# Hybrid decoder layer on one core: the fourth weight sum of a block pair moved to GpSimd, and the first key rotation moved ahead of a value block

## The chip, the core and the metric

The kernel runs on 1 core of one Trainium2 chip. A core has TensorE (PE in the profile; its weight loads are PEld), VectorE (DVE), ScalarE (ACT), GpSimd (POOL) and SyncE (SP), 16 DMA engines, an on-chip memory (SBUF) of 128 partitions and an accumulator memory (PSUM) that TensorE writes. The metric is the device time of one execution in microseconds (us), the median over several runs.

## The reference

One layer on 256 tokens of 2048 features, all in fp32. The change touches two places of it: how the weights of any large product are brought to TensorE, and the rotary step on the keys.

```python
hn = rmsnorm(h, norm_mix_w)
q, k, v, g_ret, xr, yr, g_a, g_b = split(hn @ w_in)
q = rotary(q, positions); k = rotary(k, positions) * 128 ** -0.5     # 8 heads of 128
ret = head_groupnorm(chunkwise_retention(q, k, v), ret_gn_w)         # 8 value heads of 256
ret_out = silu(g_ret) * ret
rnn_out = gelu(yr) * rg_lru(causal_dwconv(xr), ...)
merged = sigmoid(g_a) * (ret_out @ w_proj_ret) + sigmoid(g_b) * (rnn_out @ w_proj_rnn)
h = h + merged @ w_mix_out
h = h + memory_cross_attention(rmsnorm(h), rmsnorm(mem), xa_w_q, xa_w_k, xa_w_v, xa_w_o)
h = h + conv_gated_ffn(rmsnorm(h), ffn_w_up, ffn_w_down)             # inner width 5632
out = rmsnorm(h, final_norm_w)
```

## The kernel before, in words

**Weights.** Every weight matrix comes from memory in tiles of 128 partitions x 2048 numbers (four 128-row blocks by 512 columns, 1 MB). `prefetch` (L247) runs over one long list of weight units, two units ahead of the products that use them. For a unit it loads the tile (`raw`, L264, a DMA of the SP queue; six buffers), lets ACT round it to a high half (`hi`, L285) and lets DVE subtract that from the tile to get the low half (`lo`, L286); there are three buffers of each half. TensorE then multiplies with both: high activations by high weights (L361), low activations by high weights (L362), and high activations by low weights (L368), so it needs the low half only after the products with the high half.

**Pairs.** Where a product has two neighbouring 512-column blocks, `pair_products` (L384) does half of it with seven block products in place of eight, in the manner of Strassen and Winograd. Its eleven units stand in `PAIR_UNITS` (L102) in the order q1, p0, q3, p1, q5, q2, q6, p2, q7, q4, p3. The q units are the seven products; their weights are sums of tiles that are built in place, in three held tiles called A, B and C. The p units are ordinary products for the other half of the rows. The sums are:

- q1 loads A, q3 loads B, q2 loads C.
- For q5 a DMA from the POOL queue adds a tile from memory onto A (L266, an accumulating transfer). A is split into halves for q5.
- Behind that split DVE does A += B (L293, the third weight sum), and A is split again for q6.
- For q7 another accumulating DMA of the POOL queue (L266) adds a tile onto B. It has to wait for A += B, which reads B.
- Behind q6's split an entry is put into the list `after`; the next unit to be prefetched, p2, emits **A += C** (L291, the fourth weight sum) behind its own split. A is then split for q4.

There are 20 such pairs, so L291 and L293 run 20 times each, on tiles of 128 x 2048. The two last stretches of pairs are the down projections of the feed-forward layer (`pair_add`, L423). In the first pair of each, part of the activations is still being finished (`hidden`, L1260, ending in a split by ACT at L550 and DVE at L551) while its products already run.

**The first group.** The retention works on two groups of four heads (loop at L830). For group 0 the order in the code is: queries' product, value block 0 (`gemm_n`, L848), rotation of the queries (`rotated`, L708), split of value block 0 (`split_rows`, L557); then keys' product, four sums of the input (`sum_x`, L815, one behind each of the first units of the next product), value block 1, rotation of the keys, split of value block 1; then the pair of gate blocks. A rotation is eight DVE instructions (two of L715, four of L717, two of L721) and two splits (ACT L547, DVE L548). The rotated keys go to `retain` (L755), whose scores are small products (L517). A value block lies in PSUM until `split_rows` has read it (ACT L562, DVE L563); there are three such accumulators, and a pair needs all three.

**What sets the order.** Each engine works through its own queue in order. The queues are filled by a scheduler when the program is made: it takes the order of the code as priority and may put an instruction that is ready earlier ahead of one that isn't. Buffers of a pool are handed out in the order of the code.

Of the kernel before, what the change touches and what calls it, by code (L numbers as in the profile page):

```python
# [13 lines left out]
ALU = mybir.AluOpType  # L14
# [139 lines left out]
def hybrid_layer(  # L154
# [16 lines left out]
    act, dve, pe, pool, sp = nc.scalar, nc.vector, nc.tensor, nc.gpsimd, nc.sync  # L171
# [13 lines left out]
    def nm(s):  # L185
        count[0] += 1
        return f"{s}_{count[0]}"

    def big(shape, dt=F32, s="b"):
        return bp.tile(shape, dt, tag="big", name=nm(s))  # L190

    def tmp(s="t"):
        return tp.tile([P, 2, S], F32, tag="tmp", name=nm(s))
# [45 lines left out]
    def load_x(n):  # L239
        while len(xin) < n:  # L240
            t = big([P, 2, BW], s="nat")
            rows = x[0].rearrange("(t p) d -> p t d", p=P)
            c = len(xin) * BW
            act.dma_start(out=t, in_=rows[:, :, c : c + BW])
            xin.append(t)

    def prefetch(n):  # L247
        while len(ahead) < n and taken[0] < len(stream):
            kind, slot, op, i = stream[taken[0]]
            src = None if i is None else wall[i]  # L250
            taken[0] += 1
            first = taken[0] == 1
            if op == "new":
                raw = wp.tile([P, KC, BW], F32, tag="raw", bufs=RAW_BUFS, name=nm("raw"))
                if slot:
                    held[slot] = raw
            else:
                raw = held[slot]
            if taken[0] <= 4:
                xs.load(2 * taken[0] - 1)  # L260
            pieces = ((0, 1), (1, 2), (2, 4)) if first else ((0, 2), (2, 4)) if taken[0] <= 3 else ((0, 4),)
            for a, b in pieces:
                if op == "new":
                    sp.dma_start(out=raw[:, a:b, :], in_=src[:, a:b, :])  # L264
                elif op == "add":
                    pool.dma_start(out=raw, in_=src, accum_op=ALU.add)  # L266
                if first and a == 0:
                    sp.dma_start(out=xs.rest[0], in_=xs.rest[1])
                elif first and a == 1 or a == 0 and taken[0] <= 4:
                    xs.load(2 * taken[0])  # L270
            if taken[0] == 5:
                sp.dma_start(out=cid, in_=consts[:, 0:C_DEC])
                sp.dma_start(out=pa[:, 16:P], in_=by_feature[:, 16:P])
                sp.dma_start(out=pb, in_=by_feature[:, P : P + 80])
            if taken[0] == 7:
                sp.dma_start(out=pf.rearrange("p a n -> p (a n)"), in_=by_feature[:, P + 80 :])
            hi = wp.tile([P, KC, BW], F32R, tag="hi", bufs=PART_BUFS, name=nm("hi"))
            lo = wp.tile([P, KC, BW], F32R, tag="lo", bufs=PART_BUFS, name=nm("lo"))
            for a, b in pieces:
                if taken[0] <= 4:  # L280
                    xs[2 * (taken[0] - 1) + (b - 1) // KH]
                if first and b <= KH:
                    dve.tensor_copy(hi[:, a:b], raw[:, a:b])  # L283
                else:
                    act.copy(hi[:, a:b], raw[:, a:b])  # L285
                dve.tensor_tensor(  # L286
                    out=lo[:, a:b], in0=raw[:, a:b], in1=hi[:, a:b].bitcast(F32), op=ALU.subtract
                )
            if after:
                to, by = (held[i] for i in after.pop())  # L290
                dve.tensor_tensor(out=to, in0=to, in1=by, op=ALU.add)  # L291
            if kind == "q5":
                dve.tensor_tensor(out=raw, in0=raw, in1=held["B"], op=ALU.add)  # L293
            elif kind == "q6":
                after.append(("A", "C"))
            parts = [(hi[:, k : k + KH], lo[:, k : k + KH]) for k in range(0, KC, KH)]
            ahead.append((kind, parts))
            if taken[0] >= 4:
                load_x(min(4, 2 * (taken[0] - 3)))
# [3 lines left out]
    def later(n, fn):  # L303

        pending.append((step[0] + n + 1, fn))
# [64 lines left out]
    def gemm_n(w, row, st, nk, col):  # L370

        a = acc()
        for k0, parts in chunks(nk, w, row, col):
            ops = [
                [halves(st[(k0 + k) // 2], (k0 + k) % 2, slice(tt * P, (tt + 1) * P)) for k in range(KC)]
                for tt in range(2)
            ]
            for tt in range(2):
                upper_n(a[:, tt, :], ops[tt], parts, k0 == 0)
            for tt in range(2):  # L380
                lower_n(a[:, tt, :], ops[tt], parts, k0 + KC >= nk)
        return a
# [151 lines left out]
    def joined(a, s="j"):  # L534

        c = tmp("c")
        o = tmp(s)
        with tc.high_priority(URGENT):
            act.copy(c, a[:, :, S:BW])  # L539
            dve.tensor_tensor(out=o, in0=a[:, :, 0:S], in1=c, op=ALU.add)  # L540
        return o

    def split_pair(src, scale=None):

        t = big([P, 2, BW], F32R, s="s")
        if scale is None:
            act.copy(t[:, :, 0:S], src)  # L547
            dve.tensor_tensor(out=t[:, :, S:BW], in0=src, in1=t[:, :, 0:S].bitcast(F32), op=ALU.subtract)  # L548
        else:
            act.mul(t[:, :, 0:S], src, scale)  # L550
            dve.scalar_tensor_tensor(  # L551
                out=t[:, :, S:BW], in0=src, scalar=scale, in1=t[:, :, 0:S].bitcast(F32),
                op0=ALU.mult, op1=ALU.subtract,
            )
        return t

    def split_rows(a, r):  # L557

        hi, lo = (big([P, 2, BW], F32R, s="v") for _ in range(2))
        for tt in range(2):  # L560
            c = r[:, tt : tt + 1]
            act.mul(hi[:, tt, :], a[:, tt, :], c)  # L562
            dve.scalar_tensor_tensor(  # L563
                out=lo[:, tt, :], in0=a[:, tt, :], scalar=c, in1=hi[:, tt, :].bitcast(F32),
                op0=ALU.mult, op1=ALU.subtract,
            )
        return hi, lo
# [140 lines left out]
    def rotated(qs_):  # L708

        o = []  # L710
        cb = cos[:, None, :].to_broadcast([P, 2, S])
        for pr in range(2):
            q = qs_[pr]
            ta, tb = tmp("ta"), tmp("tb")
            dve.tensor_tensor(out=ta, in0=q, in1=cb, op=ALU.mult)  # L715
            for lo_, hi_ in ((0, 64), (64, 128)):
                dve.tensor_tensor(  # L717
                    out=tb[lo_:hi_], in0=q[64 - lo_ : 128 - lo_],
                    in1=sin[64 - lo_ : 128 - lo_, None, :].to_broadcast([64, 2, S]), op=ALU.mult,
                )  # L720
            dve.tensor_add(ta, ta, tb)  # L721
            o.append(split_pair(ta))
        return o
# [91 lines left out]
    def sum_x(i):  # L815

        t = tmp("xt")
        sp.dma_start(out=t, in_=x_t[:, 2 * i : 2 * i + 2, :])
        for j in range(2):
            act.activation(t[:, j, :], t[:, j, :], AF.Identity, scale=p_mix(2 * i + j))  # L820
        xs_sums.append(sums(t))
# [8 lines left out]
    for g in range(2):  # L830
        dec = big([P, 4, S], s="dec")
        vs, turned = [], []
        for b, o in enumerate((O_Q, O_K)):
            a = qjoin if g == b == 0 else [joined(t, "q") for t in gemm_t("w_in", 0, xs, NT, o + g * BW)]
            if b == 0:
                sp.dma_start(
                    out=dec,
                    in_=consts[:, C_DEC + g * 4 * S : C_DEC + (g + 1) * 4 * S].rearrange("p (h s) -> p h s", s=S),
                )
            if g > 0:  # L840
                turned.append(rotated(a))
                if b == 0:
                    vs += [split_rows(v, rs0) for v in pair_out("w_in", xs, xs_sums, O_V + 1024)]
            else:
                if b == 1:
                    for i in range(KC):
                        later(i, lambda i=i: sum_x(i))
                v = gemm_n("w_in", 0, xs, NT, O_V + b * BW)  # L848
                turned.append(rotated(a))
                vs.append(split_rows(v, rs0))  # L850
        qr, kr = turned
        gates = [head_gate(a, big([P, 2, BW], s="gate")) for a in pair_out("w_in", xs, xs_sums, O_G + g * 1024)]
        retain(g, qr, kr, vs, dec, gates)
# [418 lines left out]
    for part, nb_ in enumerate(FF_PARTS):  # L1272
# [18 lines left out]
        if final:  # L1291
            wfin = []
            for i in range(2):
                t = big([P, 2, BW], s="wf")
                sp.dma_start(
                    out=t.rearrange("p a n -> p (a n)"),
# [48 lines left out]
```

## Time and profile before

| | us |
|---|---|
| median of 3 runs (2005.9 to 2008.41) | 2006.04 |
| the profiled execution, as timed | 2005.55 |
| its span, first to last instruction | 2003.8 |
| PE busy | 1988.4 (99%) |
| DVE busy | 1583.4 (79%) |
| ACT busy | 1157.9 (58%) |
| POOL busy | 47.0 (2%) |
| DVE in the 20 sums of L291 | 45.8 |

Between the profiled execution's span and its time lie 1.75 us. A row of the trace gives the start, the duration, the engine, the line of the kernel, the operation, the tile written and the tiles read (`lo<-raw,hi`), the shape, and in square brackets how long the engine stood idle just before and what it waited for. Consecutive rows of an engine overlap by some hundredths of a microsecond. PE's matmuls are pipelined, so the duration of one (0.39) is longer than the distance between two starts (0.23 for 512 columns).

### The profile page before, as it was taken

How to read it: one execution, taken by the hardware profiler on the slowest of the kernel's cores; microseconds unless marked ns; L12 is line 12 of the kernel's file. 1: busy time of each engine (PE TensorE's matmuls, PEld its weight loads, DVE VectorE, ACT ScalarE, POOL GpSimd, SP SyncE). 2: the span in 40 equal slices, each digit the busy share in tenths (PEclk: the TensorE clock that was granted, in tenths of full speed). 3: DMA queues.
4: the chain of work that ended last, by engine and by line, in shares of the span. 5: the costliest groups of instructions: out<-in, count | busy, mean ns of one | idle time of the engine just before them, and what ended most of it. 6: DMA issues, size and time to landing. Idle time of an engine off the chain costs nothing.

```text
span 2003.8 us, 24972 instructions
## 1 busy us (share of the span) xinstructions
PE 1988.4 (99%) x10072; PEld 1692.9 (84%) x10072; DVE 1583.4 (79%) x1588; ACT 1157.9 (58%) x1167; POOL 47.0 (2%) x52
## 2 busy tenths in 40 slices
PE   9999999999999999999999999999999999999998
PEld 8878888888888888888888888888888888888887
DVE  6798797789985876778888768777797787886775
ACT  6565656767665554566666656555554554544552
POOL 0001000000000000000000000000000000000000
PEclk9999999999999999999999999999999999999999
DMA  9764675555887675777886748754678555684561
GB/s 370 259 214 135 235 257 179 210 190 157 266 261 261 210 252 183 248 257 234 267 259 206 258 126 231 264 198 174 207 233 275 196 192 216 204 290 178 204 237 64
DMA packets 79460, 443.57 MB, mean 221 GB/s; under 512 B 8688, under 2 KB 13424, under 8 KB 31600
## 3 DMA queue, kind: packets, MB, share of 16 engines
q1 hardware_dynamic: 72064, 397.39, 53.9%
q0 software_dynamic: 5760, 41.95, 11.2%
q10 hardware_dynamic: 1520, 2.63, 0.4%
q8 instruction: 79, 1.29, 0.3%
q14 instruction: 37, 0.30, 0.0%
HBM read 425.16 MB, written 16.78 MB: 221 GB/s over the span
## 4 chain that ended last, share of the span: by engine, by line
PE 91%; DVE 3%; issue 2%; DMA 2%; ACT 1%; POOLq 0%; SPq 0%; ACTq 0%; POOL 0%; DVEq 0%
PE acc L350 38%; PE acc L361 16%; PE acc L368 16%; PE acc L362 16%; DMA raw<-in_wall 2%; PE sm L517 2%; DVE lo L286 1%; PE sm L529 1%; PE acc L517 1%; ACT hi L285 1%; PE sm L894 1%; DVE raw L293 0%; DVE tb L717 0%; DVE ta L721 0%; DVE fv L1192 0%
## 5 line engine op out<-in xcount | busy, mean ns | idle before, releaser
L286 DVE TENSOR_TENSOR lo<-raw,hi 128x2048 fp32r<-128x2048 f32 (+1 forms) x420 | 951.0, 2267 | 295.0 <-ACT hi L285 288.1
L285 ACT CAST hi<-raw 128x2048 fp32r<-128x2048 f32 (+1 forms) x418 | 793.2, 1902 | 615.5 <-PE acc L362 274.2
L361 PE MATMUL acc<-hi,s 128*128 128x512 f32 x1336 | 522.6, 391 | 2.0 <-DVE v L563 1.6
L362 PE MATMUL acc<-hi,s 128*128 128x512 f32 x1336 | 520.7, 390 | 0.4 <-DVE s L551 0.4
L350 PE MATMUL acc<-s,hi 128*128 128x512 f32 x2176 | 519.3, 392 | 1.1 <-DVE hi L283 1.1
L350 PEld LDWEIGHTS acc<-s,hi 128*128 128x128 f32 x2176 | 402.7, 189 | 80.9 <-issue 1.4
L368 PE MATMUL acc<-lo,s 128*128 128x512 f32 x1336 | 340.0, 392 | 0.0
L361 PEld LDWEIGHTS acc<-hi,s 128*128 128x128 f32 x1336 | 250.9, 188 | 54.6 <-DVE v L563 2.0
L368 PEld LDWEIGHTS acc<-lo,s 128*128 128x128 f32 x1336 | 250.1, 188 | 53.3
L362 PEld LDWEIGHTS acc<-hi,s 128*128 128x128 f32 x1336 | 250.9, 188 | 52.2 <-DVE s L551 1.1
L350 PEld LDWEIGHTS acc<-s,lo 128*128 128x128 f32 x2176 | 277.7, 192 | 8.8 <-DVE lo L286 0.4
L350 PE MATMUL acc<-s,lo 128*128 128x256 f32 x2176 | 282.9, 284 | 0.0
L361 PE MATMUL acc<-hi,ss 128*128 128x512 f32 x320 | 126.4, 395 | 1.8 <-ACT o L453 1.5
L362 PE MATMUL acc<-hi,ss 128*128 128x512 f32 x320 | 124.8, 390 | 0.0
L368 PE MATMUL acc<-lo,ss 128*128 128x512 f32 x320 | 86.0, 390 | 0.0
L539 ACT COPY c<-acc 128x512 f32<-128x512 f32 x68 | 39.4, 581 | 70.3 <-PE acc L350 69.9
L361 PEld LDWEIGHTS acc<-hi,ss 128*128 128x128 f32 x320 | 60.1, 188 | 16.0 <-ACT o L453 2.0
L266 POOL DMA_DIRECT2D raw<-in_wall x40 | 35.2, 879 | 1570.3 <-DVE lo L286 999.0
L368 PEld LDWEIGHTS acc<-lo,ss 128*128 128x128 f32 x320 | 60.0, 188 | 12.7
L362 PEld LDWEIGHTS acc<-hi,ss 128*128 128x128 f32 x320 | 60.1, 188 | 12.1
L426 DVE TENSOR_TENSOR nat<-nat,acc 128x512 f32<-128x512 f32 (+1 forms) x49 | 43.9, 908 | 5.1 <-PE acc L368 5.1
L291 DVE TENSOR_TENSOR raw<-raw,raw 128x2048 f32<-128x2048 f32 x20 | 45.8, 2288 | 0.4
(233 smaller groups left out, 1241.8 us busy)
## 6 DMA issues: line engine op xcount, KB each, us to landing
raw<-in_wall SPq DMA_DIRECT2D x333, 1024.0 KB, 4.9
raw<-in_wall POOLq DMA_DIRECT2D x40, 1024.0 KB, 7.9
fkept<-nat SPq DMA_DIRECT2D x12, 512.0 KB, 7.5
nat<-fkept SPq DMA_DIRECT2D x12, 512.0 KB, 5.8
xt<-in_x_t SPq DMA_DIRECT2D x11, 256.0 KB, 6.5
raw<-in_wall SPq DMA_DIRECT2D x5, 512.0 KB, 7.9
nat<-in_x ACTq DMA_DIRECT2D x4, 512.0 KB, 10.0
ret<-hd SPq DMA_DIRECT2D x8, 256.0 KB, 4.1
```

The lines of the kernel that those rows point to most:

```text
L266: pool.dma_start(out=raw, in_=src, accum_op=ALU.add)
L285: act.copy(hi[:, a:b], raw[:, a:b])
L286: dve.tensor_tensor(out=lo[:, a:b], in0=raw[:, a:b], in1=hi[:, a:b].bitcast(F32), op=ALU.subtract)
L291: dve.tensor_tensor(out=to, in0=to, in1=by, op=ALU.add)
L350: pe.matmul(a, part, sx, start=k == 0 and t == 0, stop=k == nk - 1 and t == 0, skip_group_check=True)
L361: pe.matmul(o, h, hi, start=start and kk == 0, stop=False, skip_group_check=True)
L362: pe.matmul(o, l, hi, start=False, stop=False, skip_group_check=True)
L368: pe.matmul(o, h, lo, start=False, stop=stop and kk == KC - 1, skip_group_check=True)
L426: dve.tensor_tensor(out=o, in0=o, in1=i, op=op)
L517: pe.matmul(o, a, b, start=start and i == 0, stop=stop and i == 2, skip_group_check=True)
L529: pe.transpose(t[:, j, tt * P : (tt + 1) * P], rows[:, tt, k + j * P : k + (j + 1) * P], ident)
L539: act.copy(c, a[:, :, S:BW])
```

## The change

Two edits. The first gives the fourth weight sum, A += C, to GpSimd in place of VectorE, in all 20 pairs; its operands and its place in the code stay. The second lets group 0 rotate its keys right behind their product, ahead of the four input sums and of value block 1's product, where before the rotation stood behind that product. The queries of group 0 stay where they are.

```diff
@@ -288,7 +288,7 @@
             if after:
                 to, by = (held[i] for i in after.pop())
-                dve.tensor_tensor(out=to, in0=to, in1=by, op=ALU.add)
+                pool.tensor_tensor(out=to, in0=to, in1=by, op=ALU.add)
             if kind == "q5":
                 dve.tensor_tensor(out=raw, in0=raw, in1=held["B"], op=ALU.add)
@@ -843,10 +843,12 @@
             else:
                 if b == 1:
+                    turned.append(rotated(a))
                     for i in range(KC):
                         later(i, lambda i=i: sum_x(i))
                 v = gemm_n("w_in", 0, xs, NT, O_V + b * BW)
-                turned.append(rotated(a))
+                if b == 0:
+                    turned.append(rotated(a))
                 vs.append(split_rows(v, rs0))
```

## The prediction

> **What bounds the kernel now.** I read the page first, for which engine has no room.
>
> ```profile
> span 2003.8 us, 24972 instructions
> ...
> PE 1988.4 (99%) x10072; PEld 1692.9 (84%) x10072; DVE 1583.4 (79%) x1588; ACT 1157.9 (58%) x1167; POOL 47.0 (2%) x52
> ...
> L286 DVE TENSOR_TENSOR lo<-raw,hi 128x2048 fp32r<-128x2048 f32 (+1 forms) x420 | 951.0, 2267 | 295.0 <-ACT hi L285 288.1
> ...
> L291 DVE TENSOR_TENSOR raw<-raw,raw 128x2048 f32<-128x2048 f32 x20 | 45.8, 2288 | 0.4
> ...
> raw<-in_wall POOLq DMA_DIRECT2D x40, 1024.0 KB, 7.9
> ```
>
> PE is busy for 1988.4 of 2003.8 us, so all its idle time is 15.4 us; a change that does no less PE work can gain no more than the part of it that it removes. DVE has 79%: the 20 sums of L291 are 45.8 us of an engine that isn't the bound. Next I read PE's busy time by stretches: the first pair, two pairs in the middle, and the first pair of each of two down projections.
>
> ```profile
> core 0: us, PE busy (x) PEld busy (x) DVE busy (x) ACT busy (x) POOL busy (x), PEclk, DMA share, GB/s
> 96.60:143.30 46.70, 43.01 (x193) 35.25 (x193) 43.08 (x40) 28.25 (x26) 0.87 (x1) 1.00 0.60 203
> 645.70:686.50 40.80, 40.80 (x182) 33.78 (x180) 34.10 (x19) 25.21 (x20) 1.72 (x2) 1.00 0.68 211
> 686.50:727.30 40.80, 40.80 (x182) 33.78 (x180) 37.62 (x24) 26.98 (x24) 0.87 (x1) 1.00 0.76 247
> 1451.60:1493.70 42.10, 41.67 (x182) 33.64 (x181) 39.81 (x35) 26.56 (x21) 1.76 (x2) 1.00 0.69 227
> 1713.00:1754.90 41.90, 41.65 (x183) 33.63 (x182) 39.80 (x35) 26.57 (x21) 1.76 (x2) 1.00 0.67 230
> ```
>
> The middle pairs have PE busy in every microsecond (40.80 of 40.80): nothing can be gained there, only lost. The first pair has 46.70 - 43.01 = 3.69 us of idle PE, the largest block in the kernel behind the start. The two down pairs have 0.43 and 0.25, and DVE at 95% (39.81 of 42.10).
>
> **The change part by part: the keys.** The first pair's waits on PE are these three.
>
> ```profile
> start us, us, engine line op out<-in xcount [idle before <-releaser]
> 109.06 1.12 PE L517 MATMUL sm<-s,s 128*128 128x256 f32 x8 [0.89 <-DVE s L548]
> ...
> 111.37 0.50 PE L361 MATMUL acc<-hi,ss 128*128 128x512 f32 x1 [1.20 <-ACT o L453]
> ...
> 113.32 1.07 PE L368 MATMUL acc<-lo,ss 128*128 128x512 f32 x4
> ...
> 115.99 0.50 PE L361 MATMUL acc<-hi,s 128*128 128x512 f32 x1 [1.60 <-DVE v L563]
> ```
>
> Their sum is 0.89 + 1.20 + 1.60 = 3.69, all the idle time of that stretch. Counted by starts it is a little more: the four matmuls from 113.32 go 0.23 apart, the next was due at 114.2 and came at 115.99, 1.8 for the third. I take 4.0 for the three. All three go back to DVE:
>
> ```profile
> 78.31 0.68 DVE L540 TENSOR_TENSOR q<-acc,c 128x512 f32<-128x512 f32 x1
> ...
> 100.45 0.68 DVE L715 TENSOR_TENSOR ta<-q,cos 128x512 f32<-128x512 f32 x1
> ...
> 101.37 1.38 DVE L717 TENSOR_TENSOR tb<-q,sin 64x512 f32<-64x512 f32 x2
> ...
> 103.40 0.68 DVE L721 TENSOR_TENSOR ta<-ta,tb 128x512 f32<-128x512 f32 x1
> ...
> 108.32 0.68 DVE L548 TENSOR_TENSOR s<-ta,s 128x512 fp32r<-128x512 f32 x1
> ...
> 115.19 0.74 DVE L563 SCALAR_TENSOR_TENSOR v<-acc,ro,v 128x512 fp32r<-128x512 f32 x1
> ```
>
> The keys are complete at 78.99, and their rotation begins at 100.45, behind the four input sums. It costs 2 x (0.68 + 1.38 + 0.68 + 0.68) = 6.8 us of DVE between 100 and 112.4, ahead of value block 1's split, whose last instruction ends at 115.93; at 115.99 the matmul that wants that accumulator starts. The first wait is for rotated keys; the second is for an ACT copy (L453) that stands behind the keys' casts in ACT's queue. With the rotation ahead of the value block its 6.8 us fall between 73 and 96.6:
>
> ```profile
> 72.90:96.60 23.70, 23.70 (x110) 19.78 (x109) 14.54 (x20) 13.09 (x14) 1.04 (x1) 1.00 0.73 226
> ```
>
> DVE is idle there for 23.70 - 14.54 = 9.2 us, so the 6.8 fit, and PE has no wait in it. If that cover were thinner, a low half would come late by at most the 2.3 us that two rotation steps hold it back. No DMA moves with the rotation; the ones it now stands ahead of are the four loads of the input sums. Behind it nothing else is late: the accumulator is read some 7 us earlier. Term: **-4.0**, bounds -4.2 and 0.
>
> **The change part by part: the sums.** Removed from DVE: 20 x 2.29 us, worth nothing to PE in pairs where PE doesn't wait. Added to POOL: 20 adds of 128 x 2048, which no row shows. Two things are unknown, how long one takes and whether it gets in DVE's way. The nearest row by operation and shape is DVE's own, 2.29; on POOL the trace has only small powers:
>
> ```profile
> 193.93 5.85 POOL L609 TENSOR_TENSOR ro<-rv,mhalf 128x8 f32<-128x8 f32 x1 [3.87 <-DVE rv L607]
> ...
> 327.96 1.82 POOL L609 TENSOR_TENSOR ro<-rv,mhalf 128x8 f32<-128x8 f32 x1 [72.13 <-DVE rv L607]
> ...
> 900.79 0.72 POOL L609 TENSOR_TENSOR ro<-rv,mhalf 128x2 f32<-128x2 f32 x1 [1.31 <-DVE rv L607]
> ```
>
> From two columns to eight the power grows by 1.1 us, 0.18 a column; by that a sum would last 380 us and every pair would take ten times as long. A power is another operation than an add, so I leave that end out of the range and take 2.29, with twice that, one pass for each of the two inputs, as the upper bound. The same rows tell of the second unknown: the same power took 1.82 once and 5.85 the other time. In the long case DVE ran this:
>
> ```profile
> 193.75 2.28 DVE L286 TENSOR_TENSOR lo<-raw,hi 128x2048 fp32r<-128x2048 f32 x1
> 195.96 2.28 DVE L291 TENSOR_TENSOR raw<-raw,raw 128x2048 f32<-128x2048 f32 x1
> 198.98 2.29 DVE L286 TENSOR_TENSOR lo<-raw,hi 128x2048 fp32r<-128x2048 f32 x1 [0.74 <-ACT hi L285]
> ```
>
> Two instructions with two SBUF inputs, back to back until 198.24, then 0.74 idle; POOL ended at 199.78, 1.54 after they had ended. So POOL gets its inputs only when DVE pauses. I assume the reverse as well, that DVE's two-input work waits for a POOL add under way; no row shows it.
>
> [...]
>
> What a sum costs in a middle pair:
>
> ```profile
> 662.39 2.29 DVE L286 TENSOR_TENSOR lo<-raw,hi 128x2048 fp32r<-128x2048 f32 x1 [1.38 <-ACT hi L285]
> 664.72 2.29 DVE L291 TENSOR_TENSOR raw<-raw,raw 128x2048 f32<-128x2048 f32 x1
> 666.93 2.29 DVE L286 TENSOR_TENSOR lo<-raw,hi 128x2048 fp32r<-128x2048 f32 x1
> ...
> 669.51 1.92 ACT L285 CAST hi<-raw 128x2048 fp32r<-128x2048 f32 x1 [0.16 <-PE acc L362]
> ...
> 675.62 0.39 PE L361 MATMUL acc<-hi,ss 128*128 128x512 f32 x1
> ```
>
> q6's low half ends at 664.68. On POOL the sum then ends at 666.97, or at 669.26 if it takes twice as long; q4's cast starts at 669.51 either way, since it waits for PE to free a buffer. p2's low half starts between 666 and 669.3 in place of 666.93, and the halves are some 5 us ahead of PE (q7's is cast at 667.4, its products start at 675.62). Cost 0. The accumulating transfer for q7 is not held up: it needs A += B only, which q6's split needs too, so it is ready before the sum and I expect it ahead in POOL's queue. Behind the sum POOL has nothing until the next pair's transfer.
>
> The exceptions are the first down pairs:
>
> ```profile
> 1473.97 2.28 DVE L286 TENSOR_TENSOR lo<-raw,hi 128x2048 fp32r<-128x2048 f32 x1
> 1477.36 0.69 DVE L551 SCALAR_TENSOR_TENSOR s<-fo,s 128x512 fp32r<-128x512 f32 x1 [1.10 <-ACT s L550]
> ...
> 1735.35 2.28 DVE L286 TENSOR_TENSOR lo<-raw,hi 128x2048 fp32r<-128x2048 f32 x1
> 1738.56 0.69 DVE L551 SCALAR_TENSOR_TENSOR s<-fo,s 128x512 fp32r<-128x512 f32 x1 [0.93 <-ACT s L550]
> ...
> 1739.31 0.50 PE L362 MATMUL acc<-hi,s 128*128 128x512 f32 x1 [0.22 <-DVE s L551]
> ```
>
> PE waits for this L551 already (1739.31 follows 1739.25). DVE's pause ahead of it begins at 1737.63; a POOL sum that takes the pause ends at 1739.92 and pushes L551 from 1738.56 by 1.36. At 1476.25 likewise: 1478.54 - 1477.36 = 1.18. Cost **+2.5**, bounds 0 (nothing held) and 7.1 (twice the length: 3.65 + 3.47).
>
> Sum: -4.0 + 2.5 = -1.5 on the profiled execution's 2005.55 (1.75 around its span of 2003.8; 0.5 under the median of 2006.04): **2004.0**. A measurement here tells about 0.2%, 4 us, from no change; this is within.
>
> **The rivals.** *Nothing held:* POOL's add runs beside DVE and only the rotation counts: 2005.55 - 4.0 = 2001.5, at the edge of faster. For it: no row shows DVE held by POOL (the split at 198.98 lasted 2.29 though the power ended at 199.78). Against it: the 5.85.
>
> *The add takes twice DVE's row and holds DVE:* -4.0 + 7.1 = +3.1, 2008.6. It turns to slower by over 4 us from an add of about 5 us (both stalls then 4 each), and beyond 6 the middle pairs' cover goes too: p2's low half would end past 673 in a pair that needs it about then. For it: a power needs 0.7 us for two columns, so POOL isn't quick.
>
> *The transfer behind the sum (slower):* the place is POOL's queue. If the sum stands ahead of q7's transfer, as it does in the code, the transfer starts at 666.97, lands 7.9 later at 674.87, is cast until 676.79 and its low half is ready at 679.1, against products due at 675.62 and, with the low half, eight matmuls (1.8) later: 1.7 late. It decides as soon as the order is this one. In 18 of the 20 pairs (two have scores among their products and more room) that is 18 x 1.7 = 30 us at least: 2032 or more. Against it: DVE's queue has L291 at 664.72 ahead of p2's split at 666.93, against the code's order, so what is ready goes first.
>
> *The rotation doesn't move:* then -4.0 falls away and 2008 remains; the 6.8 us of cover speak against it.
>
> **How the numbers follow.** Forecast 0.32; nothing held 0.27; twice as long and held 0.24, a third of it past 4 us; transfer behind the sum 0.10; rotation without gain 0.07. Faster by over 0.2%: most of nothing held and a little of the forecast, 0.28. Slower: the transfer, a third to a half of the long add, some of the last, and stalls of the queues' new order that I can't see, 0.34. Within: 0.38. The range goes from 2000.8 (nothing held, -4.2 and the half microsecond of the down pairs) to 2016, an add of 6 us (4.8 + 5.1 in the down pairs by the same steps, and an estimated 5 in the middle pairs with the least cover: 2005.55 - 4.0 + 14.9); the transfer's case stays outside.
>
> **What would show it.** Right: no idle PE between 105 and 118, L715 at 73 to 90, accumulating transfers ahead of sums on POOL. The length of L291 on POOL and of L286 beside it decide between forecast and rivals: L286 rows over 2.3 us mean that DVE is held. PE's wait for L551 at the two down pairs gives the price. Wrong: PE waits at q7 or q4 in middle pairs, casts that wait for transfers, or new waits in the first 100 us.

## The result and the profile after

The changed kernel takes 2034.08 us, the median of 4 runs (2032.57 to 2039.62), against 2005.97 for the kernel before beside it: a ratio of 1.0143, 95% interval 1.0122 to 1.0164. It is slower by 28 us, where 2004.0 was forecast, and the range ended at 2016. The profiled execution lasted 2033.99 us.

The page of the changed kernel, its span, the engines' busy time and the two groups of DVE's low halves and of the moved sum (instructions x count, then busy us, mean ns, idle us before them):

```profile
span 2032.2 us, 24977 instructions
...
PE 1999.9 (98%) x10072; PEld 1699.4 (84%) x10072; DVE 1598.3 (79%) x1568; ACT 1157.6 (57%) x1167; POOL 151.7 (7%) x72
...
L286 DVE TENSOR_TENSOR lo<-raw,hi 128x2048 fp32r<-128x2048 f32 (+1 forms) x420 | 989.8, 2362 | 306.8 <-ACT hi L285 298.4
...
L291 POOL TENSOR_TENSOR raw<-raw,raw 128x2048 f32<-128x2048 f32 x20 | 106.6, 5331 | 92.8 <-DVE lo L286 89.0
```

Three readings. A sum takes 5.33 us on POOL instead of 2.29 on DVE. DVE gave up 45.8 us of sums and is busier than before, 1598.3 against 1583.4: its other instructions became longer by 60.7. And PE, with the same 10072 matmuls, is busy for 11.5 us more (1999.9 - 1988.4) and idle for 16.9 more (32.3 against 15.4). The two make up the 28.4 by which the span grew. So there are two losses: TensorE waits, and for some time it works more slowly.

The view of PE's waits of the changed kernel says for whom (total, times, longest):

```profile
PE acc L362 <- DVE s L551: 6.6, 2, 3.4
PE acc L361 <- ACT ss L505: 3.2, 1, 3.2
PE sm L529 <- ACT hd L752: 2.6, 1, 2.6
...
PE acc L368 <- DVE lo L286: 1.8, 1, 1.8
```

**A POOL sum and DVE's work with two SBUF inputs exclude each other.** Rows of the changed kernel's timeline, first a sum that found DVE idle, with the low half that started 0.59 us later:

```profile
721.03 4.61 POOL L291 TENSOR_TENSOR raw<-raw,raw 128x2048 f32<-128x2048 f32 x1 [2.97 <-DVE lo L286]
...
721.62 6.17 DVE L286 TENSOR_TENSOR lo<-raw,hi 128x2048 fp32r<-128x2048 f32 x1 [0.68 <-ACT hi L285]
...
941.21 4.61 POOL L291 TENSOR_TENSOR raw<-raw,raw 128x2048 f32<-128x2048 f32 x1 [3.65 <-DVE lo L286]
...
941.36 4.62 DVE L503 TENSOR_TENSOR sm<-xt,sm 128x128 f32<-128x128 f32 x1
```

The sum ends at 725.64, the low half at 727.79: 2.15 later, about its usual 2.28. It did nothing while the sum ran. The second couple is plainer: a DVE add of 128 columns, 0.28 to 0.29 us in the kernel before, needs 4.62, to just behind the sum's end. The other order:

```profile
268.16 2.28 DVE L286 TENSOR_TENSOR lo<-raw,hi 128x2048 fp32r<-128x2048 f32 x1
...
268.33 6.62 POOL L291 TENSOR_TENSOR raw<-raw,raw 128x2048 f32<-128x2048 f32 x1 [3.03 <-DVE lo L286]
...
123.09 4.86 POOL L291 TENSOR_TENSOR raw<-raw,raw 128x2048 f32<-128x2048 f32 x1 [10.54 <-DVE lo L286]
...
123.39 0.74 DVE L786 BATCH_NORM_STATS2 bn<-rc 128x6 f32<-128x256 f32 x2
```

Where DVE is first, POOL waits: the sum of 268.33 lasts 6.62 and ends 4.5 behind the low half. The statistics at 123.39, which have one input, run inside a sum in their usual 0.41 each. The sum's own length is thus 4.6 (the shortest of the 20 is 4.60, the median 4.63).

**Half clock.** In the first pair of the first down projection (PE's, POOL's and DVE's rows, then busy time by stretches, where the sixth number is the granted clock):

```profile
1492.23 7.11 POOL L291 TENSOR_TENSOR raw<-raw,raw 128x2048 f32<-128x2048 f32 x1 [5.65 <-DVE lo L286]
...
1496.21 3.68 DVE L551 SCALAR_TENSOR_TENSOR s<-fo,s 128x512 fp32r<-128x512 f32 x1 [1.26 <-ACT s L550]
...
1499.95 0.50 PE L362 MATMUL acc<-hi,s 128*128 128x512 f32 x1 [3.22 <-DVE s L551]
...
1501.43 0.63 PE L361 MATMUL acc<-hi,s 128*128 128x512 f32 x1
1501.86 0.63 PE L362 MATMUL acc<-hi,s 128*128 128x512 f32 x1
```
```profile
1500.90:1504.30 3.40, 3.40 (x10) 2.66 (x9) 3.40 (x3) 0.45 (x2) 0.00 (x0) 0.51 0.92 383
1504.30:1508.00 3.70, 3.70 (x17) 3.02 (x17) 2.39 (x3) 1.84 (x1) 0.00 (x0) 0.99 1.01 427
```

DVE is ready for L551 at 1496.21, the sum holds it until 1499.34, and TensorE waits 3.2 us. Behind that the matmuls start 0.43 apart instead of 0.23, for 3.4 us, at a granted clock of 0.51. The trace's clock record has five such stretches inside the kernel after, each 3.41 us or twice that, 23.9 us in all, and none before. At half speed that is about 12 us of work, the 11.5 of PE's busy time.

**Two more places.** In the second pair (at 170 in the kernel before) the power of the retention's norm stands behind the sum in POOL's queue; its result is wanted by the gate, the heads and TensorE in turn:

```profile
197.18 6.66 POOL L291 TENSOR_TENSOR raw<-raw,raw 128x2048 f32<-128x2048 f32 x1 [3.79 <-DVE rv L607]
203.80 3.73 POOL L609 TENSOR_TENSOR ro<-rv,mhalf 128x8 f32<-128x8 f32 x1
...
207.56 0.36 DVE L798 TENSOR_SCALAR ro<-ro,ro 128x4 f32<-128x4 f32 x2 [0.97 <-POOL ro L609]
...
216.00 1.38 PE L529 MATMUL sm<-cid,rc 128*128 128x128 f32 x8 [2.65 <-ACT hd L752]
```

It ended at 207.53, in the kernel before at 199.78. Of these 7.75 us the first pair had already lost 3.3; the other 4.4 are the sum's. And in the pair at 476, four scans that stood behind four low halves more in DVE's queue before (at 516.47, 2.43 us for the four) now stand ahead of p2's low half, where room had come, and are held by POOL:

```profile
509.77 5.62 POOL L291 TENSOR_TENSOR raw<-raw,raw 128x2048 f32<-128x2048 f32 x1 [7.61 <-DVE lo L286]
...
510.93 6.76 DVE L919 TENSOR_TENSOR_SCAN xr<-aa,ti 128x256 f32<-128x256 f32 x4
...
518.19 2.28 DVE L286 TENSOR_TENSOR lo<-raw,hi 128x2048 fp32r<-128x2048 f32 x1
...
520.53 1.88 PE L368 MATMUL acc<-lo,s 128*128 128x512 f32 x5 [1.80 <-DVE lo L286]
```

**The keys.** The loads of the input sums on SP's queue, the last of these sums, and TensorE in the first pair, all of the kernel after:

```profile
64.72 14.28 SPq L264 DMA_DIRECT2D raw<-in_wall  x4
79.05 0.43 SPq L818 DMA_DIRECT2D xt<-in_x_t  x1
...
89.63 0.68 DVE L548 TENSOR_TENSOR s<-ta,s 128x512 fp32r<-128x512 f32 x1
90.23 0.28 DVE L500 TENSOR_TENSOR sm<-xt 128x128 f32<-128x128 f32 x1
...
112.03 0.69 DVE L506 TENSOR_TENSOR ss<-sm,ss 128x512 fp32r<-128x512 f32 x1 [0.15 <-ACT ss L505]
...
108.39 0.49 PE L362 MATMUL acc<-hi,ss 128*128 128x512 f32 x1 [0.57 <-DVE ss L506]
112.05 0.80 PE L361 MATMUL acc<-hi,ss 128*128 128x512 f32 x1 [3.16 <-ACT ss L505]
```
```profile
111.70:118.50 6.80, 6.45 (x15) 4.76 (x16) 5.45 (x8) 4.26 (x6) 0.86 (x1) 0.50 0.79 149
```

The rotation runs where it was forecast, 79.2 to 90.3, and the old waits for L548, L453 and L563 are gone. But the input sums begin only behind it, at 90.23 (82.88 before), their loads start at 79.05 in place of 72.28, and the fourth sum is complete at 112.72 rather than 103.47. The two rows of the kernel before:

```profile
72.28 0.43 SPq L818 DMA_DIRECT2D xt<-in_x_t  x1
...
102.78 0.69 DVE L506 TENSOR_TENSOR ss<-sm,ss 128x512 fp32r<-128x512 f32 x1
```

q3, the pair's third product, multiplies with these sums (`ss`): 3.7 us of waits again, now followed by 6.8 us at half clock.

How much later the same matmul starts than in the kernel before, by stretches of that kernel's time (us gained or lost within each; the experiments' columns are used below):

| stretch, in the time of the kernel before | after | `sum_only` | `sum_pieces` | `sum_spared` | `sum_eleven` |
|---|---|---|---|---|---|
| start and first pair, to 169.5 | 3.3 | 0.3 | -0.2 | 0.2 | 1.7 |
| second pair, to 237 | 6.1 | 5.9 | 7.6 | 5.9 | 0.5 |
| third pair, to 306 | 1.3 | 1.3 | 1.7 | 1.3 | 0.3 |
| pairs at 476 to 602, to 645.7 | 4.0 | 5.3 | 6.2 | 7.6 | 0.0 |
| to 905 | 0.0 | 0.0 | 1.0 | 0.0 | 0.0 |
| to 1036 | 1.1 | 0.5 | 4.4 | 1.0 | 0.0 |
| pairs of two cross-attention products, to 1180 | 2.8 | 3.0 | 7.8 | 2.9 | 0.0 |
| to 1451.6 | 0.0 | 0.0 | 2.1 | 0.0 | 0.0 |
| first down projection, to 1535 | 4.0 | 5.0 | 2.2 | -0.3 | -0.3 |
| second down projection, to the end | 5.5 | 5.7 | 2.7 | 0.5 | 0.5 |
| all | 28.2 | 27.1 | 35.5 | 19.2 | 2.7 |

### The profile page after: what moved, and what is told of

Read it like the earlier page. It is cut to its first block, busy times and chain, and to the rows that moved or that the text cites. A ratio compares the mean times of both kernels' runs of the same rounds, so it can differ in the third digit from the quotient of the medians.

```text
span 2032.2 us, 24977 instructions
## 1 busy us (share of the span) xinstructions
PE 1999.9 (98%) x10072; PEld 1699.4 (84%) x10072; DVE 1598.3 (79%) x1568; ACT 1157.6 (57%) x1167; POOL 151.7 (7%) x72
## 4 chain that ended last, share of the span: by engine, by line
PE 87%; DVE 6%; issue 3%; DMA 2%; ACT 1%; POOL 1%; SPq 0%; POOLq 0%; ACTq 0%; DVEq 0%
PE acc L350 36%; PE acc L361 16%; PE acc L362 16%; PE acc L368 16%; DVE lo L286 2%; DMA raw<-in_wall 1%; PE sm L517 1%; ACT hi L285 1%; PE sm L529 1%; PE sm L896 1%; PE acc L517 0%; DVE raw L293 0%; DVE s L551 0%; POOL raw L291 0%; DVE xr L919 0%
## 5 line engine op out<-in xcount | busy, mean ns | idle before, releaser
L286 DVE TENSOR_TENSOR lo<-raw,hi 128x2048 fp32r<-128x2048 f32 (+1 forms) x420 | 989.8, 2362 | 306.8 <-ACT hi L285 298.4
L291 POOL TENSOR_TENSOR raw<-raw,raw 128x2048 f32<-128x2048 f32 x20 | 106.6, 5331 | 92.8 <-DVE lo L286 89.0
L368 PEld LDWEIGHTS acc<-lo,ss 128*128 128x128 f32 x320 | 60.7, 190 | 13.0
```

What stands on the lines that cost most here:

```text
L286: dve.tensor_tensor(out=lo[:, a:b], in0=raw[:, a:b], in1=hi[:, a:b].bitcast(F32), op=ALU.subtract)
L291: pool.tensor_tensor(out=to, in0=to, in1=by, op=ALU.add)
L368: pe.matmul(o, h, lo, start=False, stop=stop and kk == KC - 1, skip_group_check=True)
```

## The experiments

The theory: the sum on POOL and DVE's two-input work exclude each other, and what is late by it costs in a few pairs, with half clock behind the longer waits; the keys' rotation makes the input sums late. The rivals: the loss is the sum's own lateness or POOL's slowness; it runs through all pairs; the clock drops for another reason than idling; the rotation's place itself is at fault.

**`sum_only`: the first edit alone.**

```diff
-                dve.tensor_tensor(out=to, in0=to, in1=by, op=ALU.add)
+                pool.tensor_tensor(out=to, in0=to, in1=by, op=ALU.add)
```

> The fourth weight sum on GpSimd alone, the keys rotated where they were before. Theory (hold): one add of 4.6 us keeps out every VectorE instruction with two SBUF inputs while it runs, so this part costs most of the change: about 23 us over before, near 2029 us. It shows low-half splits stretched from 2.28 to 5 or 6 us, waits of TensorE for L551 of some 3.5 us in the first pair of each down projection, and half-clock stretches behind them. Rival (the two edits meet): the loss needs both edits in the first pairs, and the sums alone cost the two down pairs only, about 10 us, 2016 us.

2033.03 us (2032.08 to 2035.34), ratio 1.0132, 1.0115 to 1.0149. That is 4 us more than worked out, and far from the rival's 2016: the sum is nearly the whole loss. The two waits for L551 are the same as after (6.3 us together).

**`keys_only`: the second edit alone** (the second part of the change's diff).

> The keys rotated ahead of value block 1 alone, sums on VectorE. Theory (late input sums): the rotation takes the place of the four input sums in the queues and buffers, the fourth input sum comes some 9 us later, TensorE waits for it at the third product of the first gate pair: about 5 us slower than before, 2011 us. Rival (the forecast's step): the three waits of 3.7 us vanish, 4 us faster, 2002 us, and what was seen in the first pair of the changed kernel came from the sums on GpSimd.

2008.84 (2008.31 to 2009.52), ratio 1.0010, 1.0001 to 1.0020. A small loss, just clear of the noise and smaller than worked out, in place of a gain of 4. The two losses added are 26.36 + 2.17 = 28.5 us, against 28.1 for both edits together.

**`keys_xtbig`: the second edit, the input tiles of the sums in another buffer pool**, so that their loads don't wait for a small temporary.

```diff
-        t = tmp("xt")
+        t = big([P, 2, BW], s="xt")[:, :, 0:S]
```

> As the keys alone, but the four input tiles of the input sums lie in the pool of large buffers and not among the ten temporaries that the rotation uses. If the input sums are late because their loads wait for a temporary behind the rotation's, the loads start as before (72 to 84 us), the fourth input sum is ready by about 105 us and the time is 4 us under before, 2002 us. If it is VectorE's time and queue order that delays them, the time stays near that of the keys alone, 2011 us.

2009.55 (2008.74 to 2012.24), ratio 1.0015, 1.0006 to 1.0025. The last input sum starts at 112.21, no earlier. The buffer isn't what holds the loads back. They stand behind one weight load more in SP's queue (the x4 above was x3 in the kernel before), and the sums' DVE part stands behind the rotation.

**`sums_then_keys`: the second edit, the input sums hung into the keys' own product**, one product earlier.

```diff
+            if g == 0 and b == 1:
+                for i in range(KC):
+                    later(i, lambda i=i: sum_x(i))
             a = qjoin if g == b == 0 else [joined(t, "q") for t in gemm_t("w_in", 0, xs, NT, o + g * BW)]
...
                 if b == 1:
-                    for i in range(KC):
-                        later(i, lambda i=i: sum_x(i))
+                    turned.append(rotated(a))
                 v = gemm_n("w_in", 0, xs, NT, O_V + b * BW)
-                turned.append(rotated(a))
+                if b == 0:
+                    turned.append(rotated(a))
```

> Sums on VectorE; the four input sums behind the first units of the keys' own product, the keys' rotation ahead of value block 1. Theory (late input sums): with the input sums out of the way the rotation's place is worth what was forecast: no wait of TensorE between 105 and 118 us, about 4 us faster than before, 2002 us. Rival (VectorE has no room): the work only moves, VectorE's splits for value block 1 come late, no gain or a loss.

2001.57 (2001.25 to 2003.68), ratio 0.9974, 0.9963 to 0.9984: faster than both kernels. The stretch of the first pair, the last rotated keys and the last input sum:

```profile
96.60:143.30 46.70, 46.70 (x214) 38.96 (x213) 38.93 (x23) 29.22 (x22) 0.87 (x1) 1.00 0.80 250
```
```profile
88.23 0.69 DVE L506 TENSOR_TENSOR ss<-sm,ss 128x512 fp32r<-128x512 f32 x1
...
97.27 0.69 DVE L548 TENSOR_TENSOR s<-ta,s 128x512 fp32r<-128x512 f32 x1
```

PE is busy in all of the 46.70 us. This is the gain of 4 that was forecast for the keys.

**`sums_early_keys_late`: the input sums as there, the rotation where it was**, behind value block 1 (of that diff the three lines that hang in the input sums, and their old three lines taken out; the rotation's lines stay as in the kernel before).

> The sums on DVE. The four input sums are put into the keys' own product, as in the faster version of the keys' part, but the rotation of the keys stays behind value block 1, where it was. If the gain of that version comes from the rotation's place, this one gains nothing: 2005.5 to 2007. If it comes from the input sums being out of the rotation's way (in the kernel before, the rotation begins at 100.45 only because the last input sum ends there), most of the gain is here too: 2001.5 to 2003.5, and the waits for L548 and L563 are gone with the rotation still in its old place.

2001.84 (2001.12 to 2003.87), ratio 0.9980, 0.9971 to 0.9990. The same gain with the rotation not moved in the code; PE is again busy in all of the 46.70 us from 96.60. The rotation's first instruction:

```profile
85.54 0.69 DVE L715 TENSOR_TENSOR ta<-q,cos 128x512 f32<-128x512 f32 x1
```

With the input sums gone, the rotation starts at 85.54 by itself rather than at 100.45. What kept the keys late in the kernel before were the input sums ahead of them in DVE's queue; to move those earlier is the whole gain, and the second edit as made only turned the two around.

**`sum_pieces`: the sum on POOL in four adds of 512 columns.**

```diff
-                dve.tensor_tensor(out=to, in0=to, in1=by, op=ALU.add)
+                for k in range(KC):
+                    pool.tensor_tensor(out=to[:, k], in0=to[:, k], in1=by[:, k], op=ALU.add)
```

> The keys' rotation as before; the sum A += C on POOL, in four adds of 128 x 512 instead of one of 128 x 2048. Hold theory (a POOL add and a two-input DVE instruction don't run beside each other, and whichever starts first holds the other until it ends): a piece is about 4.6 / 4 = 1.2 us, so DVE is held by at most about 1.2 us at a time; the wait for L551 in the first pair of each down projection falls from 3.4 to at most 1.3 us, no half clock follows it, the two pairs cost some 1 to 3 us in place of 5.6 each, and the time is 2010 to 2022. Rival (the sum is late or POOL is simply slow, so that A's split for q4 is what TensorE waits for): four adds are no shorter than one, the waits stay or grow, and the time is 2031 or more.

2041.76 (2038.42 to 2042.61), ratio 1.0174, 1.0157 to 1.0191: the time was expected wrongly, the length of the waits rightly, and the half clock wrongly, since a stretch of 3.41 us follows in both down pairs. Its group of sums, PE at the first down projection (L552 and L551 are L551 and L550 of the kernel before), and ACT's waits for the sums:

```profile
L292 POOL TENSOR_TENSOR raw<-raw,raw x80: 1260/1298/3866, 120.2 to 1815.3; 128x512 f32<-128x512 f32 x80
```
```profile
1508.37 0.50 PE L362 MATMUL acc<-hi,s 128*128 128x512 f32 x1 [0.56 <-ACT s L551]
1509.88 0.51 PE L363 MATMUL acc<-hi,s 128*128 128x512 f32 x1 [1.00 <-DVE s L552]
```
```profile
ACT hi L285 <- POOL raw L292: 39.8, 14, 6.0
```

A piece alone takes 1.26 to 1.30 us, and the wait for L551 falls from 3.2 to 1.0; the two down projections cost 2.2 and 2.7 instead of 5.0 and 5.7. That is the hold, instruction by instruction. But between its pieces POOL itself is held by DVE, so that a piece lasts up to 3.87 us: a sum needs 8.1 us (161.8 in 20), q4's cast waits for it in 14 pairs (39.8 us; 11.2 in 5 pairs after), and pairs that cost nothing before now do. The rival's mechanism, a late sum, is real too: with pieces it costs more than the shorter hold saves.

**`sum_spared`: POOL in 18 pairs, DVE in the first pair of each down projection.** The added lines note these two units of the plan in a set `spared`, and the sum's engine is chosen by it.

```diff
+                eng = dve if taken[0] in spared else pool
-                dve.tensor_tensor(out=to, in0=to, in1=by, op=ALU.add)
+                eng.tensor_tensor(out=to, in0=to, in1=by, op=ALU.add)
```

> The keys as before; the sum on POOL in 18 pairs, and on DVE in the first pair of each of the two paired down projections. Theory that each pair has its own loss: the 5.6 and 5.7 us of these two pairs go, with their waits for L551 and the half clock behind them, and the time is 2033.0 - 11.3 = 2021.7 (2020 to 2024). Rival (the lost time sits in how the clock or the queues run over the whole stretch, and only shows there first): the next pair pays in their place and the time stays above 2028.

2022.75 (2021.45 to 2025.18), ratio 1.0084, 1.0069 to 1.0099. The two pairs' loss goes with the two sums, and the pairs behind them don't take it over. The profiled execution took 2025.18: it has a half-clock stretch, behind a wait of 2.22 us at 563, that `sum_only` doesn't have. This makes the 7.6 in the table.

**`sum_eleven`: POOL only in the eleven pairs that lost nothing in `sum_only`** (the set holds the nine others).

> The keys as before; the sum on POOL only in the eleven pairs that cost nothing when all twenty were moved, on DVE in the nine others. If each pair's loss is its own, and DVE's 2.3 us are worth nothing where they are freed: 2006 +- 1, no change, with 25 us of adds moved to POOL. If moving the sum gains something in the quiet pairs that the losses of the others hid, it is faster than before, 2004 or less; if the losses only move on to the pairs that still have the sum on POOL, 2015 or more.

2006.77 (2006.26 to 2008.50), ratio 1.0001, 0.9992 to 1.0011: no difference.

```profile
L299 POOL TENSOR_TENSOR raw<-raw,raw 128x2048 f32<-128x2048 f32 x11 | 50.8, 4616 | 44.3 <-DVE lo L293 44.3
...
L299 DVE TENSOR_TENSOR raw<-raw,raw 128x2048 f32<-128x2048 f32 x9 | 20.6, 2287 | 0.1
```

Eleven sums on POOL cost nothing, and the 25 us that DVE is spared buy nothing. The 1.7 us at this kernel's start in the table arose before 15, in a half-clock stretch at 11.8, ahead of all sums. So each pair has its own loss, and no gain elsewhere stands against it.

**`sum_fill`: `sum_only`, with ten matmuls of zero weights in TensorE's queue in these two pairs.**

```diff
             pe.matmul(o, h, hi, start=start and kk == 0, stop=False, skip_group_check=True)
+            if fill and kk == 2:
+                for _ in range(10):
+                    pe.matmul(o, none, hi, start=False, stop=False, skip_group_check=True)
```

The lines that set `none` to zero and set `fill` for one product of each of the two pairs are left out here.

> The sums on POOL, the keys as before, and ten matmuls with weights of nothing (2.27 us at 0.227 a matmul) put into TensorE's queue just ahead of the matmul that waits for L551 in the first pair of each down projection; they add zero to an accumulator. Idle-gap theory (TensorE is granted half clock for 3.41 us or twice that behind a grid window in which it stood idle for some 2 us): DVE's split still ends when it did, the rest of the wait is 3.45 - 2.27 = 1.2 us, no half clock follows in either pair, and with 6.83 us at half clock saved twice, at half their length, the time is 2033.0 - 6.8 = 2026.2 (2025 to 2028). Rival (the clock drops for what POOL and DVE draw or for something else than TensorE's idling): the half clock stays where it was, and the time is 2032 to 2034.

2030.13 (2027.35 to 2032.03), ratio 1.0116, 1.0101 to 1.0131. That lies between the two expectations. The matmuls stand not just ahead of the waiting one but some 16 us earlier, in p1's product (from 1484.26), and this changed the order of the held work too. In `sum_only` the sum waits for a low half that DVE runs without a pause, lasts 7.11 us and holds the split (L551 there, L555 here). Here DVE pauses for 0.17 us ahead of that low half; the sum takes the pause, lasts 5.00, and holds the low half (6.47 us), and the split runs behind it in its usual 0.68. So the wait is shorter by 1.5 us, for both reasons together. Its rows, then the same 6.8 us at half clock in `sum_only` and the stretch behind the wait here:

```profile
1501.97 0.50 PE L365 MATMUL acc<-hi,s 128*128 128x512 f32 x1 [1.68 <-DVE s L555]
1502.30 0.40 PE L361 MATMUL acc<-hi,s 128*128 128x512 f32 x1
1502.54 0.39 PE L365 MATMUL acc<-hi,s 128*128 128x512 f32 x1
```
```profile
1496.50:1503.30 6.80, 5.68 (x13) 4.47 (x14) 6.07 (x4) 2.48 (x2) 0.52 (x1) 0.50 0.76 290
```
```profile
1501.90:1505.30 3.40, 3.33 (x15) 2.76 (x16) 3.40 (x4) 0.51 (x1) 0.00 (x0) 1.00 1.01 422
```

The wait is 1.68 and no half clock follows, in either pair. POOL and DVE do the same instructions as in `sum_only`, in a slightly other order, and hold each other as before; what is gone is part of TensorE's idling. That idling brings the half clock is borne out by the windows of all traces (last section). By the start of the same matmuls, as in the table, the two stretches lose 2.4 and 3.2 us instead of 5.0 and 5.7, with 4.5 us of added work. The saving of 5.0 is less than the expected 6.8, since part of each half-clock stretch lay in the wait itself (PE busy in 5.68 of 6.80). In the profiled execution (2032.03) some 4 us of it are lost again: 2.2 at 520 to 563, where the clock dropped, as in `sum_spared` and not in `sum_only`, and 2.2 between 905 and 1036, where it didn't.

## Why the prediction was wrong

- **The sum's length.** "I take 2.29", DVE's row, was wrong; the upper bound of twice that was right (4.60), though that an add makes one pass for each of its inputs, the reason given for it, is shown by no run. The power of eight columns says nothing of an add.
- **Whether POOL and DVE exclude each other.** Assumed, and right, in both directions. That POOL gets its inputs "only when DVE pauses" is too narrow: of the 6.62 us of the sum of 268.33 the last 4.6 begin at 270.35, and DVE shows no pause there (its low half ends at 270.44, L865 starts at 270.36 and is held). What was not drawn from it: the sum waits as well, so one that meets a low half under way lasts 6.6 to 7.1 us (six of the 20).
- **The down pairs.** The mechanism and place were right. The stalls worked out for twice the length, 3.65 and 3.47, came as 3.65 and 3.49 us between the starts; by the table the two stretches cost 5.5 and 4.0, and what goes beyond the stalls is half clock.
- **The step that failed most: "Cost 0" in a middle pair, with the first down pairs as the only exceptions.** It was read from one pair, at 646, and holds in eleven of the twenty. Beside the two down pairs seven more lose time, where the stage's own small work is in the same queues: the retention's power behind the sum on POOL (6.1), the scans in DVE's freed place (most of 4.0), smaller ones in the third pair and the cross-attention (1.3, 1.1, 2.8). Together some 15 of 28 us.
- **Half clock behind a wait** was in no term. It makes about 12 of the 28 us, spread over the places above. In the kernel before no wait was followed by it, and the prediction took a wait to cost its length.
- **The keys, -4.0.** "The 6.8 fit" was right, and so was that the three waits go. "Behind it nothing else is late" failed: the input sums are. "No DMA moves" failed with it, the four loads moved by 6.8 us and more. The term was +2.2 to +3.3. The -4.0 is what the three waits are worth, and it came once the input sums were earlier, with the rotation moved (`sums_then_keys`) or not (`sums_early_keys_late`): the step read the rotation's place as the cause, and the cause was the input sums ahead of it.
- **The transfer ahead of the sum in POOL's queue** was right; that rival fell. "Nothing held" fell with the 6.17 us row. The second rival, twice as long and held, had the right mechanism at 2008.6. It missed the keys (some 7 us), the seven pairs and the half clock.

What is argued from rows and not tried: that the second pair's 6 us come from the power's place behind the sum (without that sum in `sum_eleven` the loss is 0.5, but this takes the hold away as well), and why the scheduler put one weight load more ahead of the input tiles. The smaller losses, in the third pair and the cross-attention, were not followed up one by one.

## What to carry to other kernels

An engine with 2% load isn't free room. See from a trace whether it excludes the busy engine (a sum of 4.6 us held DVE for up to 4.4 us here: 0.17 became 4.62), and price the move in every stage that has it, by what stands next in both queues there: one quiet pair showed 0, seven others lost 15 us. When an instruction is moved ahead of others, ask when the displaced ones are wanted; here the displaced sums were wanted sooner, and to move those gave the gain instead. TensorE waits of 2.22 us (`sum_spared`, at 563) to 3.2 us (after, at 1499.95) in a dense stretch cost, beside their length, half of the next 3.41 us or of twice that.

## What the runs showed of the hardware

TensorE's clock fell to half behind some 2 us of idling. The stretches last 3.41 us or twice that, and lie on a grid of 3.41 us within one execution: in the clock record of the kernel after they begin at 111.72, 217.53, 521.32, 1500.94 and 1763.77, which is 31, 89, 287 and 77 times 3.4133 apart, and the only shares it has are 1.0 and 0.5. Waits of 2.65 and of 3.2 us were followed by one; so were two of 0.56 and 1.00 us 1.5 us apart in `sum_pieces`, some 2 us between the starts. 1.68 in `sum_fill` was not. A wait of 1.80 was followed by one after (at 520.53) and not in `sum_only`, where it stood elsewhere on the grid; one of 2.12 in `sum_fill` (at 517.23), which a border of the grid cut in two, wasn't either. So in these traces it is the idling within one window of the grid that counts. The eleven traces, between 20 and 2015 us, can be cut into such windows, and the idling counted as what lies between matmul starts beyond their usual spacing. All 17 windows that began at full clock and held 2.13 us or more of it were followed by half clock, none with 1.97 or less, and two of the three in between (2.09 to 2.12).

A DVE instruction of 0.28 us can last 4.62 behind a POOL add (L503 above), and one of 0.17 us on 16 columns (L865) lasted as long at 270.36. These short two-input instructions lose most by it in proportion (a low half takes 6.17 at most, against 2.28), and the profile books the time as DVE's busy time, not as a wait.
